# A hybrid diffusion block on one core: the seventh pair's output splits and weights one by one, the first query weights split earlier, a shorter chain in the norms

## The chip, the cores and the metric

The kernel runs on one core of a Trainium2 chip. The metric is the device time of one execution in microseconds (us). Before the change it is 1886.7 us, the median of three runs (1886.16 to 1886.85). Five engines work beside each other: TensorE (PE in the profile; its weight loads are PEld), VectorE (DVE), ScalarE (ACT), GpSimd (POOL), and the queue SP that issues the transfers.

## The reference, cut to what matters

Two layers over 512 latent tokens and a prefix of 256 context tokens, all in float32, D_MODEL 1024: attention with QK-norm, a ConvFFN, a bidirectional SSD mixer, a second ConvFFN. Ahead of each sub-layer stands an RMSNorm with shift and scale:

```python
def rms_norm(x, g):
    y = xf * lax.rsqrt(jnp.mean(xf * xf, axis=-1, keepdims=True) + EPS)
h_l = modulate(rms_norm(x, norm_mix_w[i]), mod_l[0], mod_l[1])
# attention: 16 heads of 64, 4 key-value heads; latent queries see all 768 keys, context queries 256
s = jnp.einsum('bqhgd,bkhd->bhgqk', q, k) * (HEAD_DIM ** -0.5)
p = jax.nn.softmax(s, axis=-1)
o_l = ob.reshape(bsz, seq, Q_DIM) @ w_o
x = x + mod_l[2] * o_l
x = x + mod_l[5] * conv_ffn(h_l, ffn_w_up[i], ...)
```

mod_l and mod_c come from SiLU(cond) through a linear map per layer (adaLN).

## The kernel before

**Numbers and splits.** Channels lie on partitions and tokens along the rows: a tile of X is 128 channels by 512 latent or 256 context tokens. Each float32 factor of a product is split into a high part, cast by ScalarE (`split`, L85), and a low part, the difference, taken by VectorE or GpSimd (L87). A product is three matmuls: high by high (L105), high by low activations (L106), low weights by high (L108). `load_w` fetches a weight tile of 128x1024 (wst) and splits it into wh and wl.

**Order of work.** In attention the order on TensorE, ScalarE and VectorE comes from a planner of the tile framework, which starts from the order in which the code issues the work; matmuls, casts and sums of different generators are interleaved by hand. `Fill` is a queue of generators of side work: run(us) takes from it until so many microseconds of TensorE's time are spent. `spread(us)` does the same for `stream()`, which holds ten items: four query projections for pairs 4 to 7 (`qproj`) and six blocks of adaLN products (ps_ada).

**Attention.** Sixteen heads are eight pairs. For a pair, `maxima()` makes scores in one rounding (ps_m) and takes their maxima (L610, ma, mb); from these comes a diagonal matrix diag (L631). `steps()` has seven steps, t = 0 to 6: scores ps_s (L680, with diag L682 subtracting the maxima), exp on ScalarE (pr, L683), sums of pr (acc, L688 and L690), and one step later the products with the values (ps_o, L644; in the context part ps_oc). ps_s and ps_m share a PSUM pool of two tiles, so the scores of a step wait for the exp, or the maximum, two tiles earlier. A pair ends with o = ps_o / ps_sum (L653 to L657), and pairs 0 to 5 park o in DRAM. The maxima of pair p+1 run beside the steps of pair p. `values()` is the stretch ahead of the pairs: products of v with the first maxima between them. `osplit(p)` fetches a parked o and splits it (hhol, hlol of 512 columns; hhoc, hloc of 256), and `project(fs)` multiplies it by w_o (ps_d) as side work. In the seventh pair (p = 6), at t = 0, five osplits are issued one after another, then `late()`, which loads the five w_o tiles in its projections.

**Norms.** `Norm.sq` squares a tile (L325) and adds it to one of two sums; the last tile (m = 7) adds to one (L330) and then adds the other (L332). `rstd_rows` sums over channels on TensorE (ss, L236), takes Ln and Exp on ScalarE (L241), improves the root on VectorE (L243, L244), spreads it to 128 columns per block of tokens (rb, L247) and transposes that on TensorE (rsT, L253), so that each partition has the row of roots. `Norm.gen` copies the row out of PSUM (rs, L345), and `modulated` (ht L281, hh L290, hl L291) makes the eight normed tiles of a segment of 256 tokens. Norm names: a (before attention, own code), f (before both FFNs), s (before the SSD layer). Segments: three for the first f and for s, two for the last f, eight in all.

Of the kernel before, what the change touches and what calls it, by code (L numbers as in the profile page):

```python
# [80 lines left out]
def split(g, src, hi, lo, lo_engine="dve", pin=False):  # L81

    nc = g.nc
    keep = g.tc.keep_in_program_order if pin else lambda i: i
    keep(nc.scalar.copy(hi, src))  # L85
    eng = nc.vector if lo_engine == "dve" else nc.gpsimd
    keep(eng.tensor_tensor(lo, src, _r(hi), ALU.subtract))  # L87


# [131 lines left out]


def ln_exp(g):
    follow(g, g.nc.scalar.preload_act_table_set("natural_log_exp_and_others"))


def rstd_rows(g, sq, n, cols, width, name, bank):
# [19 lines left out]
    nc.vector.scalar_tensor_tensor(rb.rearrange("p (a b) -> p a b", b=P // c), wide(u), 1.5, wide(y), ALU.add, ALU.mult)  # L247
    yield BREAK
    out = []
    for t0 in range(0, nt, 4):  # L250
        pt = bank(f"rsT{name}")
        for t in range(t0, min(nt, t0 + 4)):
            nc.tensor.transpose(pt[:, (t - t0) * P : (t - t0 + 1) * P], rb[:, t * P : (t + 1) * P], g.ident)  # L253
        yield (pt, t0 * P, min(n, (t0 + 4) * P))
# [55 lines left out]
class Norm:  # L310
# [8 lines left out]
    def sq(self, seg, x, m):  # L319

        i, a, b = seg
        nc = self.g.nc
        sq = t3(self.g, f"sq{self.name}", n=b - a)
        for ap, c0, c1 in parts(x[i][m], a, b):
            nc.scalar.activation(sq[:, c0:c1], ap, AF.Square)  # L325
# [4 lines left out]
        (nc.vector if m == 7 else nc.gpsimd).tensor_tensor(acc, acc, sq, ALU.add)  # L330
        if m == 7:
            nc.vector.tensor_tensor(acc, acc, self.acc[seg, 0], ALU.add)  # L332

    def gen(self, seg, x, lag=2):
# [7 lines left out]
        for _ in range(lag):  # L342
            yield
        rs = t3(g, f"rs{self.name}", n=n)
        nc.scalar.copy(rs, next(rows)[0][:, :n])  # L345
        for m in range(KT):
# [33 lines left out]
def attention(g, fill, X, late):  # L380
# [177 lines left out]
    qraw = {p: raw[j] for p, j in ((0, 1), (1, 2), (2, 4), (3, 5))}  # L558

    def qproj(p):  # L560

# [3 lines left out]
        w = t4(g, "wh", F32R), t4(g, "wl", F32R)  # L565
        split(g, st, *w, lo_engine="pool")
        yield
        qs = qraw[p] = t3(g, "qs")
        for h, c0, n in ((hc, L, C), (hl, 0, L)):
            ps = Bk("ps_q")  # L570
            for k in range(KT):
                ks = slice(k * P, (k + 1) * P)
                mm3(g, (w[0][:, ks], w[1][:, ks]), [(ps[:, :n], h[k])], k == 0, k == KT - 1)
                yield 3 * n / 2400
            nc.scalar.copy(qs[:, c0 : c0 + n], ps[:, :n])

    def queries(p, eng):
# [13 lines left out]
    class Pair:  # L591
# [43 lines left out]
        def steps(self):  # L635
# [37 lines left out]
            for t in range(7):  # L673
                ps, pr = Sb("ps_s"), g.t3p.tile([P, 1024], F32, tag="pr", bufs=3, name="pr")
                for q0, n, k0, off in (((0, L, t * P, 0),) if t < 6 else ((L, C, L, 0), (L, C, L + P, C))):
# [5 lines left out]
                    for e in range(2):  # L681
                        nc.tensor.matmul(outs[e], onesr[S64[e]], self.diag[S64[e], q], start=False, stop=True)  # L682
                nc.scalar.activation(pr, ps, AF.Exp)  # L683
                if t == 0:
# [34 lines left out]
    odram = [g.dp.tile([P, T], F32, name=f"odram{p}") for p in range(6)]  # L719

    def osplit(p):
        hl_, hc_ = htiles(g, L, f"ol{p}"), htiles(g, C, f"oc{p}")
        o = g.o[p]
        if p < 6:
            o = t3(g, f"od{p}")
            nc.sync.dma_start(o, odram[p])
        split(g, o[:, :L], *hl_)
        split(g, o[:, L:T], *hc_)
        g.oT.append((hl_, hc_))
# [5 lines left out]
    def stream():  # L735
# [38 lines left out]
    for i, _ in enumerate(vals):  # L774
# [4 lines left out]
        if i in (12, 26, 30, 34):  # L779
            next(qgen[2], None)  # L780
        if i == 20:
            next(side)
    for gen in (m, qgen[1], qgen[2]):
        for _ in gen:
            pass
    late_step = None
    for p in range(NH // 2):
        m = iter(())
        if p < 7:
            m = pairs[p + 1].maxima()  # L790
        if p == 6:
            for _ in side:
                pass
            for _, gen in tails:
                for _ in gen:
                    pass
        for t, todo in enumerate(pairs[p].steps()):
# [9 lines left out]
            if p == 7 and t == 3:  # L807
                osplit(5)
                osplit(6)
# [502 lines left out]
def body(nc, tc, I, out, dbg=None):  # L1312
# [37 lines left out]

    def project(fs):

        ws = [load_w(g, I["w_o"][f * P : (f + 1) * P]) for f in fs]
        yield 0
        for i in range(2):
# [3 lines left out]

    def late():  # L1360
        for fs in ((0, 1, 2), (3, 4), (5, 6, 7))[:-1]:
            fill.add(project(fs))

# [136 lines left out]
```

## Time and profile before

| | |
|---|---|
| median of three runs | 1886.7 us (1886.16 to 1886.85) |
| profiled execution | 1888.97 us |
| its span, first to last instruction | 1887.2 us |
| mean granted TensorE clock | 0.997 |
| TensorE busy | 1857.0 us, 98% |
| VectorE busy | 1315.0 us, 70% |
| ScalarE busy | 811.3 us, 43% |
| GpSimd busy | 303.5 us, 16% |
| transfers | 211.67 MB, mean 112 GB/s |

The span is what the trace covers; the execution's time also holds 1.8 us around it. The profiled execution is 2.3 us above the median. "Busy" counts the time in which an engine has an instruction in work; a busy TensorE may run at a lower granted clock (1.00 is full). A line's number is that of the kernel before; the changed kernel's lines have other numbers (L85 and L87 stay, L105 is L106, L247 is L252, L281 is L292, L610 is L625, L631 is L646, L690 is L705).

### The profile page before, as it was taken

Reading aid. Unit: us, or ns where it says so; the run is one execution under the profiler, and the core shown is the slowest. Engines: PE = TensorE matmul, PEld = TensorE weight load, DVE = VectorE, ACT = ScalarE, POOL = GpSimd, SP = SyncE. Lnnn points to the kernel's source line nnn. Section 1 sums busy time; section 2 is a strip of 40 time slices with the busy share of each in tenths; the row PEclk is TensorE's granted clock in tenths of the full one; section 3 lists DMA queues with packets and bytes.
Section 4 is the critical chain, followed back from the end, with each engine's and each line's share of the span. In section 5 each row is a group of like instructions: output and inputs, shape, how many; then the busy total and the mean of one; then the engine's idle time right before and its main releaser. Section 6 shows DMA issues by size and latency. Waiting matters only on the chain.

```text
span 1887.2 us, 28798 instructions
## 1 busy us (share of the span) xinstructions
PE 1857.0 (98%) x11474; PEld 1549.0 (82%) x11474; DVE 1315.0 (70%) x1950; ACT 811.3 (43%) x1410; POOL 303.5 (16%) x266
## 2 busy tenths in 40 slices
PE   9999999999999999999999999999999999999999
PEld 7866655688888888888888888888888888888887
DVE  6578887687877776444487877777787476565655
ACT  3534443363222222222367667776666252323331
POOL 2132120040000000000031334444333210000000
PEclk9999999999999999999999999999999999999999
DMA  9232151115434553122224324343453222323232
GB/s 342 78 117 87 63 179 50 50 41 201 140 129 140 195 176 116 55 67 68 67 90 131 117 88 117 113 124 123 123 157 105 74 95 95 101 85 106 90 101 90
DMA packets 74070, 211.67 MB, mean 112 GB/s; under 512 B 9040, under 2 KB 14544, under 8 KB 73808
## 3 DMA queue, kind: packets, MB, share of 16 engines
q1 hardware_dynamic: 73936, 209.84, 33.9%
q8 instruction: 90, 1.47, 0.3%
q14 instruction: 44, 0.36, 0.1%
HBM read 198.79 MB, written 6.82 MB: 109 GB/s over the span
## 4 chain that ended last, share of the span: by engine, by line
PE 80%; DVE 11%; issue 4%; POOL 2%; ACT 2%; DMA 1%; SPq 0%; DVEq 0%; POOLq 0%; ACTq 0%
PE ps_up L106 10%; PE ps_up L108 10%; PE ps_up L105 10%; PE ps_d L105 6%; PE ps_d L106 6%; PE ps_d L108 6%; PE ps_in L108 4%; PE ps_in L106 4%; PE ps_in L105 4%; PE ps_s L680 2%; PE ps_o L644 2%; PE ps_st L1090 1%; DVE wl L87 1%; DVE ht L281 1%; DVE xf L1020 1%
## 5 line engine op out<-in xcount | busy, mean ns | idle before, releaser
L87 DVE TENSOR_TENSOR wl<-wst,wh 128x1024 fp32r<-128x1024 f32 x207 | 261.0, 1261 | 229.9 <-PE ps_up L106 141.9
L85 ACT CAST wh<-wst 128x1024 fp32r<-128x1024 f32 x211 | 221.3, 1049 | 398.4 <-DMA wst<-in_wup 322.0
L106 PE MATMUL ps_up<-hlf,wh 128*128 128x512 f32 (+1 forms) x1008 | 357.4, 355 | 0.0
L108 PE MATMUL ps_up<-hhf,wl 128*128 128x512 f32 (+1 forms) x1008 | 357.2, 354 | 0.0
L105 PE MATMUL ps_up<-hhf,wh 128*128 128x512 f32 x1008 | 357.2, 355 | 0.0
L105 PEld LDWEIGHTS ps_up<-hhf,wh 128*128 128x128 f32 x1008 | 190.6, 189 | 26.4
L106 PEld LDWEIGHTS ps_up<-hlf,wh 128*128 128x128 f32 x1008 | 190.8, 189 | 26.2
L108 PEld LDWEIGHTS ps_up<-hhf,wl 128*128 128x128 f32 x1008 | 190.7, 189 | 26.3
L105 PE MATMUL ps_in<-hhs,wh 128*128 128x512 f32 (+1 forms) x560 | 204.6, 365 | 1.2 <-ACT dt L975 1.2
L106 PE MATMUL ps_in<-hls,wh 128*128 128x512 f32 (+1 forms) x560 | 199.6, 356 | 0.0
L108 PE MATMUL ps_in<-hhs,wl 128*128 128x512 f32 (+1 forms) x560 | 199.0, 355 | 0.0
L105 PE MATMUL ps_d<-hdh,wh 128*128 128x512 f32 (+1 forms) x568 | 193.6, 343 | 0.3 <-ACT hdh L85 0.2
L108 PE MATMUL ps_d<-hdh,wl 128*128 128x512 f32 (+1 forms) x568 | 193.5, 341 | 0.0
L106 PE MATMUL ps_d<-hdl,wh 128*128 128x512 f32 (+1 forms) x568 | 193.0, 340 | 0.3 <-DVE hdl L87 0.3
L841 DVE SCALAR_TENSOR_TENSOR X<-ps_d,mod,X 128x512 f32<-128x512 f32 (+1 forms) x224 | 124.6, 583 | 37.1 <-PE ps_d L108 36.8
L105 PEld LDWEIGHTS ps_in<-hhs,wh 128*128 128x128 f32 x560 | 106.0, 189 | 16.3 <-ACT dt L975 1.4
L106 PEld LDWEIGHTS ps_d<-hdl,wh 128*128 128x128 f32 x568 | 106.7, 188 | 14.7 <-DVE hdl L87 0.7
L108 PEld LDWEIGHTS ps_in<-hhs,wl 128*128 128x128 f32 x560 | 105.9, 189 | 14.8
L105 PEld LDWEIGHTS ps_d<-hdh,wh 128*128 128x128 f32 x568 | 106.4, 188 | 13.6 <-ACT hdh L85 0.6
L108 PEld LDWEIGHTS ps_d<-hdh,wl 128*128 128x128 f32 x568 | 106.8, 188 | 13.1
L106 PEld LDWEIGHTS ps_in<-hls,wh 128*128 128x128 f32 x560 | 106.1, 189 | 13.2
L683 ACT ACTIVATE pr<-ps_s 128x1024 f32<-128x1024 f32 x56 | 57.2, 1021 | 105.2 <-PE ps_s L682 105.1
(344 smaller groups left out, 3679.7 us busy)
## 6 DMA issues: line engine op xcount, KB each, us to landing
wst<-in_wup SPq DMA_DIRECT2D x88, 512.0 KB, 3.3
wada<-in_adaT SPq DMA_DIRECT2D x56, 512.0 KB, 3.3
wst<-in_win SPq DMA_DIRECT2D x48, 512.0 KB, 3.4
wst<-in_wdown SPq DMA_DIRECT2D x44, 512.0 KB, 3.7
E<-ad SPq DMA_DIRECT2D x64, 256.0 KB, 6.1
wada<-in_adaB SPq DMA_DIRECT2D x24, 512.0 KB, 4.4
ec<-ead SPq DMA_DIRECT2D x64, 128.0 KB, 5.5
wst<-in_wout SPq DMA_DIRECT2D x16, 512.0 KB, 3.3
```

The lines of the kernel that those rows point to most:

```text
L85: keep(nc.scalar.copy(hi, src))
L87: keep(eng.tensor_tensor(lo, src, _r(hi), ALU.subtract))
L105: mm(out, wh, ah, start=first, stop=False)
L106: mm(out, wh, al, start=False, stop=False)
L108: mm(out, wl, ah, start=False, stop=last)
L281: nc.vector.scalar_tensor_tensor(t[:, c0:c1], ap, g.moda[layer][ca][:, m, v : v + 1], rs[:, c0:c1], ALU.mult, ALU.mult)
L644: nc.tensor.matmul(po[S64[e], :n], v, pr[:, 512 * e + off : 512 * e + off + n], start=first, stop=last)
L680: nc.tensor.matmul(outs[e], kk[e][a][S64[e], k], b[S64[e], q], start=i == 0, stop=False)
L683: nc.scalar.activation(pr, ps, AF.Exp)
L841: nc.vector.scalar_tensor_tensor(ap, o[:, c0:c1], gate[:, m, v : v + 1], ap, ALU.mult, ALU.add)
L1020: i = nc.vector.scalar_tensor_tensor(cv, raw[:, tap : tap + n], par(f"sw{tap}", j), cv, ALU.mult, ALU.add)
L1090: nc.tensor.matmul(ps[:, d * 256 : (d + 1) * 256], Bt[:, t * P : (t + 1) * P], xw[d][t], start=t == ts[0], stop=t == ts[-1])
```

## The change

Three things are changed. **First**, `stream()`'s second item, the query projection of pair 4, gets its cast and its low part during the values' stretch (at i == 30; the side work is started at i == 16 instead of 20); the casts of the other three query weights are kept behind the newest exp by an ordering without a semaphore. **Second**, in pair 6 one osplit, one fetch of the next o and one w_o tile are issued per step, t = 0 to 4; the projections are added at t = 2 (three) and t = 4 (two). In pair 5 and in steps 0 to 2 of pair 6 the stream is spent with 0.62 us per step (1.04 before), what is left of it at t = 2 of pair 6; from then on Fill.run gets 3.5 us per step (2.9 before). **Third**, where a row has one column per token block (c == 1), the improved root stays 128x(blocks) and TensorE's transpose reads it as a broadcast operand; the copy out of PSUM is gone, and ht reads the row there; for m == 7 the two older sums are added before the last square.

```diff
@@ split
-    keep(nc.scalar.copy(hi, src))
+    cast = keep(nc.scalar.copy(hi, src))
...
+    return cast
...
+def behind(g, bi, other):
+    g.tc.add_manual_dep(bi.ins, other.ins.name, mybir.DependencyInfo(
+        mybir.DependencyClass.NoSync, mybir.DependencyReason.DATA), reason="kept behind")
...
@@ rstd_rows
-    rb = t3(g, f"rb{name}", n=n)
-    wide = lambda v: v.unsqueeze(2).broadcast_to([P, nt * c, P // c])
-    nc.vector.scalar_tensor_tensor(rb.rearrange("p (a b) -> p a b", b=P // c), wide(u), 1.5, wide(y), ALU.add, ALU.mult)
+    if c == 1:
+        nc.vector.scalar_tensor_tensor(a, u, 1.5, y, ALU.add, ALU.mult)
+        root = lambda t: a[:, t : t + 1].broadcast_to([P, P])
+    else:
...
-            nc.tensor.transpose(pt[:, (t - t0) * P : (t - t0 + 1) * P], rb[:, t * P : (t + 1) * P], g.ident)
+            nc.tensor.transpose(pt[:, (t - t0) * P : (t - t0 + 1) * P], root(t), g.ident)
@@ Norm.sq, Norm.gen
-        (nc.vector if m == 7 else nc.gpsimd).tensor_tensor(acc, acc, sq, ALU.add)
         if m == 7:
             nc.vector.tensor_tensor(acc, acc, self.acc[seg, 0], ALU.add)
+        (nc.vector if m == 7 else nc.gpsimd).tensor_tensor(acc, acc, sq, ALU.add)
...
-        rs = t3(g, f"rs{self.name}", n=n)
-        nc.scalar.copy(rs, next(rows)[0][:, :n])
+        rs = next(rows)[0][:, :n]
@@ attention, qproj
-        split(g, st, *w, lo_engine="pool")
+        cast = split(g, st, *w, lo_engine="pool")
+        if exps:
+            behind(g, cast, exps[-1])
@@ attention, osplit and the values' stretch
+    def ofetch(p):
+        od[p] = t3(g, f"od{p}")
+        nc.sync.dma_start(od[p], odram[p])
...
-            if i + 1 < len(items) and i + 1 in (1, 3, 4, 5):
+            if i + 1 in (3, 4, 5):
                 next(items[i + 1])
...
-        if i == 20:
+        if i == 16:
             next(side)
+        if i == 30:
+            next(items[1])
@@ attention, the pairs
-        if p == 6:
-            for _ in side:
-                pass
...
-            if t == 0:
-                if p == 6:
-                    for i in range(5):
-                        osplit(i)
-                    late()
...
-                spread(1.04)
+                    if p == 5:
+                        ofetch(0)
+                spread(1.04 if p < 5 else 0.62)
+                continue
+            if p == 6 and t < 5:
+                if t < 4:
+                    ofetch(t + 1)
+                osplit(t)
+                wos.append(load_w(g, I["w_o"][t * P : (t + 1) * P]))
+            if p == 6 and t == 2:
+                late(wos[:3], (0, 1, 2))
+            if p == 6 and t == 4:
+                late(wos[3:], (3, 4))
+            if p == 7 and t == 2:
+                ofetch(5)
...
+            if p == 6 and t < 3:
+                spread(0.62)
+                if t == 2:
+                    for _ in side:
+                        pass
...
             else:
-                fill.run(2.9)
+                fill.run(3.5)
```

**GpSimd at the start of the pairs.** Three ropes (L534 to L536 before, L544 to L546 now; raw_901 before and raw_899 now are the sixth tile of raw queries and keys) and the low parts wl of the query weights. Before, three wl in a row stand behind the third rope:

```order
L534 TENSOR_TENSOR raw_903<-raw_903,cs 128x512
L535 TENSOR_TENSOR qsw<-qsw,cs 128x512
L536 TENSOR_TENSOR raw_903<-raw_903,qsw 128x512
L87 TENSOR_TENSOR wl<-wst,wh 128x1024 x3
L534 TENSOR_TENSOR raw_901<-raw_901,cs 128x512
```

Now:

```order
L87 TENSOR_TENSOR wl<-wst,wh 128x1024
L544 TENSOR_TENSOR raw_901<-raw_901,cs 128x512
L545 TENSOR_TENSOR qsw<-qsw,cs 128x512
L546 TENSOR_TENSOR raw_901<-raw_901,qsw 128x512
L544 TENSOR_TENSOR raw_899<-raw_899,cs 128x512
```

The first wl moved ahead of a rope, and two wl stand behind the last rope of raw.

**VectorE around the seventh pair's diag.** accc is the sum of pair 5's last exp, mz the smaller of the maxima, od a fetched o. Before:

```order
L694 TENSOR_TENSOR accc<-pr 128x512
L626 TENSOR_TENSOR mz<-ma,mb 64x6 x4
L87 TENSOR_TENSOR wl<-wst,wh 128x1024
L631 TENSOR_TENSOR diag_3262<-id_918,mz 128x6x64 x2
L655 TENSOR_TENSOR o_2939<-ps_o,y 128x512
L656 SCALAR_TENSOR_TENSOR u<-ps_sum,y 128x512
L610 TENSOR_REDUCE ma<-ps_m 128x2x2
```

Now:

```order
L709 TENSOR_TENSOR accc<-pr 128x512
L641 TENSOR_TENSOR mz<-ma,mb 64x6 x4
L646 TENSOR_TENSOR diag_3223<-id_916,mz 128x6x64 x2
L87 TENSOR_TENSOR hlol_3316<-od_3238,hhol_3315 128x512
L670 TENSOR_TENSOR o_2937<-ps_o,y 128x512
L671 SCALAR_TENSOR_TENSOR u<-ps_sum,y 128x512
L133 STREAM_TRANSPOSE ada_tr<-ps_ada 128x128
L672 SCALAR_TENSOR_TENSOR o_2937<-u,o_2937 128x512
L87 TENSOR_TENSOR hloc_3318<-od_3238,hhoc_3317 128x256
L87 TENSOR_TENSOR hlol_3351<-od_3313,hhol_3350 128x512
L625 TENSOR_REDUCE ma<-ps_m 128x2x2
```

The wl ahead of diag is gone from there, and two low parts of o and an adaLN transpose now stand between diag and the next maximum.

**ScalarE in the last segment's norm before the second FFN.** Before:

```order
L325 ACTIVATE sqf_14796<-x_13858 128x256
L85 CAST wh<-wst 128x1024
L241 ACTIVATE rsy<-rsa 128x2
L241 ACTIVATE rsy<-rsy 128x2
L345 COPY rsf_14842<-rsTf_14843 128x256
L290 ACTIVATE hhf_0_14371<-ht,mod_95 128x256
```

Now:

```order
L336 ACTIVATE sqf_14772<-x_13838 128x256
L247 ACTIVATE rsy<-rsa 128x2
L85 CAST wh<-wst 128x1024
L247 ACTIVATE rsy<-rsy 128x2
L301 ACTIVATE hhf_0_14350<-ht,mod_95 128x256
```

The weight cast moved from ahead of Ln to between Ln and Exp, and the copy is gone.

More of the change, by code (lines that the diff above doesn't have):

```diff
@@ L244, in rstd_rows @@
     nc.vector.scalar_tensor_tensor(u, y, -0.5, u, ALU.mult, ALU.mult)
-    rb = t3(g, f"rb{name}", n=n)
-    wide = lambda v: v.unsqueeze(2).broadcast_to([P, nt * c, P // c])
-    nc.vector.scalar_tensor_tensor(rb.rearrange("p (a b) -> p a b", b=P // c), wide(u), 1.5, wide(y), ALU.add, ALU.mult)
+    if c == 1:
+        nc.vector.scalar_tensor_tensor(a, u, 1.5, y, ALU.add, ALU.mult)
+        root = lambda t: a[:, t : t + 1].broadcast_to([P, P])
+    else:
+        rb = t3(g, f"rb{name}", n=n)
+        wide = lambda v: v.unsqueeze(2).broadcast_to([P, nt * c, P // c])
+        nc.vector.scalar_tensor_tensor(rb.rearrange("p (a b) -> p a b", b=P // c), wide(u), 1.5, wide(y),
+                                       ALU.add, ALU.mult)
+        root = lambda t: rb[:, t * P : (t + 1) * P]
     yield BREAK
-    out = []
     for t0 in range(0, nt, 4):
@@ L558, in attention @@
     qraw = {p: raw[j] for p, j in ((0, 1), (1, 2), (2, 4), (3, 5))}
+    exps = []
     def qproj(p):
@@ L575, in qproj @@
             nc.scalar.copy(qs[:, c0 : c0 + n], ps[:, :n])
+        qraw[p] = qs
     def queries(p, eng):
@@ L682, in steps @@
                         nc.tensor.matmul(outs[e], onesr[S64[e]], self.diag[S64[e], q], start=False, stop=True)
-                nc.scalar.activation(pr, ps, AF.Exp)
+                exps.append(nc.scalar.activation(pr, ps, AF.Exp))
                 if t == 0:
@@ L815, in attention @@
                         pass
-                spread(1.04)
+                    if p == 5:
[13 more added lines that the diff above has]
+                ofetch(5)
+            if p == 7 and t == 3:
+                osplit(5)
+                osplit(6)
+            if p == 6 and t < 3:
[3 more added lines that the diff above has]
+                        pass
+                    for _, gen in tails:
+                        for _ in gen:
+                            pass
             else:
-                fill.run(2.9)
+                fill.run(3.5)
     late_step()
@@ L1349, in body, with project @@
     x = [[X[:, m, a:b] for m in range(KT)] for a, b in ((0, L), (L, T))]
-    def project(fs):
-        ws = [load_w(g, I["w_o"][f * P : (f + 1) * P]) for f in fs]
-        yield 0
+    def project(fs, ws):
         for i in range(2):
@@ L1358, in project, with late @@
                 yield 3 * len(fs) * streams[i][0] / 2400
-    def late():
-        for fs in ((0, 1, 2), (3, 4), (5, 6, 7))[:-1]:
-            fill.add(project(fs))
+    def late(ws, fs):
+        fill.add(project(fs, ws))
     attention(g, fill, X, late)
```

14 lines of the change are left out of this document (3 added, 11 removed).

## The prediction

> **What bounds the kernel now.** First the page's totals of busy time, then the windows table (span cut into stretches; columns: length, busy time of TensorE's matmuls, its weight loads, VectorE, ScalarE and GpSimd with their counts, granted TensorE clock, DMA share, GB/s):
>
> ```profile
> span 1887.2 us, 28798 instructions
> PE 1857.0 (98%) x11474; PEld 1549.0 (82%) x11474; DVE 1315.0 (70%) x1950; ACT 811.3 (43%) x1410; POOL 303.5 (16%) x266
> 110.00:130.00 20.00, 18.12 (x168) 12.35 (x167) 14.96 (x16) 6.86 (x10) 9.25 (x5) 0.91 0.51 172
> 130.00:258.00 128.00, 128.00 (x930) 77.67 (x929) 102.46 (x146) 57.58 (x80) 24.98 (x14) 1.00 0.23 74
> 258.00:310.00 52.00, 46.81 (x424) 27.81 (x422) 47.00 (x79) 24.92 (x38) 4.80 (x3) 0.97 0.46 164
> 385.00:435.00 50.00, 47.99 (x361) 45.04 (x360) 39.88 (x83) 30.56 (x69) 19.18 (x23) 1.00 0.26 95
> 930.00:990.00 60.00, 55.74 (x435) 52.53 (x435) 43.98 (x97) 36.95 (x85) 20.99 (x25) 1.00 0.23 80
> 1500.00:1530.00 30.00, 26.24 (x207) 24.43 (x205) 21.66 (x45) 14.35 (x34) 4.60 (x5) 1.00 0.21 70
> ```
>
> TensorE is the bound: 98% over the span, no gap at all in 130 to 258. So what TensorE gains early reaches the end, and the change can win only where TensorE idles: 1.9 us in 110 to 130, 5.2 in 258 to 310, 2.0 in 385 to 435, 4.3 in 930 to 990, 3.8 in 1500 to 1530. The clock column holds more: it is below 1 in just two of these rows. Cut finer:
>
> ```profile
> 122.00:124.00 2.00, 2.00 (x12) 0.57 (x8) 1.02 (x2) 1.66 (x2) 1.13 (x1) 0.59 0.01 4
> 124.00:126.00 2.00, 2.00 (x8) 1.22 (x7) 2.00 (x2) 0.00 (x0) 1.22 (x1) 0.56 0.01 4
> 292.00:294.00 2.00, 1.71 (x8) 0.80 (x8) 2.00 (x4) 1.02 (x1) 0.00 (x0) 0.76 0.00 0
> 294.00:296.00 2.00, 2.00 (x5) 1.00 (x6) 1.86 (x5) 0.80 (x2) 0.00 (x0) 0.50 0.01 4
> 296.00:298.00 2.00, 2.00 (x12) 0.91 (x10) 1.40 (x4) 0.84 (x1) 0.00 (x0) 0.89 0.05 20
> ```
>
> The first two rows lose 2x(0.41+0.44) = 1.7 us to the slow clock, the other three 2x(0.24+0.50+0.11) = 1.7 us. TensorE counts as fully busy there, so no wait shows this cost. Each stretch follows a stall, so a stall's price can be its idle time plus 1.7 us.
>
> **Part A, the first query weights.** Timeline rows (start, length, engine; idle before and releaser in brackets):
>
> ```profile
> 113.94 1.28 POOL L534 TENSOR_TENSOR raw<-raw,cs 128x512 f32<-128x512 f32 x1 [13.03 <-ACT pr L683]
> 118.58 2.34 POOL L87 TENSOR_TENSOR wl<-wst,wh 128x1024 fp32r<-128x1024 f32 x1
> 118.81 0.28 PE L106 MATMUL ps_q<-hla,wh 128*128 128x256 f32 x1
> 120.97 0.39 PE L108 MATMUL ps_q<-hha,wl 128*128 128x256 f32 x1 [1.88 <-POOL wl L87]
> ```
>
> GpSimd does a rope (three operations from 113.94 on) first and the low part wl behind it. The changed order puts wl ahead of that rope, and its cast into the values' stretch, where GpSimd had been idle for 13.03 us. Then the wait goes: 120.97-118.81 = 2.16 us from start to start, less the product's own 0.28: 1.9. The slow clock behind it goes too, since no other wait is listed in 110 to 130: 1.7. **A = 3.6.** Lower bound 1.1: the clock loss stays, and wl at its new place costs VectorE something; nearest is the operation that it ends up beside (VectorE's diag of 1.02 us, below, doubled at worst, of which I count 0.8). Nothing else waits for the casts pushed behind the last exp: TensorE has no idle time in 130 to 258.
>
> [...]
>
> **Part B, pairs six and seven of the eight (258 to 310).** The rows in order of time; the first is pair six's diag part of the scores, the second the end of pair five's ctx sums:
>
> ```profile
> 260.05 0.50 PE L682 MATMUL ps_s<-diag,onesr 64*128 64x512 f32 x2 [0.71 <-DVE diag L631]
> 261.63 0.60 PE L650 MATMUL ps_oc<-accc,ones 128*64 128x256 f32 x4
> 266.83 1.08 PE L644 MATMUL ps_o<-pr,v 128*64 128x512 f32 x4
> 269.19 1.08 PE L644 MATMUL ps_o<-pr,v 128*64 128x512 f32 x4
> 270.20 1.95 PE L129 MATMUL ps_ada<-wada,sc 128*32 128x128 f32 x64
> 282.02 0.50 PE L608 MATMUL ps_m<-khs,qh 64*128 64x512 f32 x1 [1.17 <-DVE ma L610]
> 285.27 0.38 PE L680 MATMUL ps_s<-qh,kh 64*128 64x256 f32 x1 [1.74 <-ACT pr L683]
> 290.07 1.23 DVE L87 TENSOR_TENSOR wl<-wst,wh 128x1024 fp32r<-128x1024 f32 x1
> 291.21 1.02 DVE L631 TENSOR_TENSOR diag<-id,mz 128x384 fp32r<-128x384 f32 x2
> 292.29 0.50 PE L682 MATMUL ps_s<-diag,onesr 64*128 64x512 f32 x2 [1.57 <-DVE diag L631]
> 294.35 1.22 PE L105 MATMUL ps_d<-hhol,wh 128*128 128x512 f32 x2
> 296.05 0.68 DVE L87 TENSOR_TENSOR hlol<-od,hhol 128x512 fp32r<-128x512 f32 x1
> ```
>
> VectorE sets the pace here: 47.00 of 52 us busy. A wide operation takes 1.14 from start to start (290.07 to 291.21), 0.09 less than its length; a step takes TensorE 2.36 when nothing waits (266.83 to 269.19). The change takes wl from in front of the seventh pair's diag and puts one adaLN block (1.95) ahead of that pair's first scores. So the diag wait, 1.57, goes. The block at 270.20 is the one that moves, so both engines can run up to 1.95 earlier from there and the wait for ma falls from 1.2 to about 0.6; the wait for pr stays at 1.7 to 1.9, because its exp stands behind a cast that waits for VectorE. With the part of the slow clock before 294.35 (0.7) and the spacings around the stalls, my schedule by hand has the ctx sums end at 290.7 instead of 294.35: 3.6 earlier.
>
> Behind that the cost comes. The products with w_o (ps_d), which filled TensorE between the seventh pair's steps, now stand behind the scores of step 3. In its new order VectorE must do, from diag to the maximum that step 3 waits for: 3 maxima, 2 sums and one wl (6 at 1.14 = 6.8); three hlol, a last one excepted, and three rows of o, u, o of 512 columns (6 at 0.6, from hlol's 0.68 = 3.6); three hloc and three rows of 256 (6 at 0.34, hloc's 0.42 below = 2.0); small ones 0.6: 13.0 us. TensorE has for it 2.2, from the diag part to the end of the ctx sums (260.05 to 262.23, one pair earlier), and three steps of 2.36, 9.3 in all, of which 0.5 follows the last wait. New idle time: 13.0-8.8 = 4.2. Before, between 294.35 and 304.65, TensorE did 24 ps_d (5.5 at full clock) and one step (2.4), 7.9 us of work in 10.3: it lost 2.4 there. So 3.6-4.2+2.4 = 1.8. I take off half of one slow stretch (0.85 to 0.9), as three gaps of 1.1 to 1.7 follow each other within 10 us. **B = 0.9.** Bounds: -1.6 (two slow stretches, 3.4) and +6.2 (waits of 1.2+1.7+1.6 and the clock's 1.7 all gone, none new). The fetches of o and the w_o loads come one per step instead of all at once; at over 2.36 us a step they stay hidden behind the step before.
>
> **Part E, end of attention.**
>
> ```profile
> 379.74 0.42 DVE L87 TENSOR_TENSOR hloc<-o,hhoc 128x256 fp32r<-128x256 f32 x1
> 380.21 0.38 PE L106 MATMUL ps_d<-hloc,wh 128*128 128x256 f32 x1 [0.63 <-DVE hloc L87]
> ```
>
> The larger filling per step (3.5 for 2.9) and the earlier projection put one group of 24 ps_d more behind the last sums, each of 0.1 us at least, which is over three times the wait. **E = 0.6**, bounds 0 and 0.8 (a second small wait stands before it).
>
> **Part N, the norms.** First the row of the kernel's first norm, then the last segment before the second FFN, which shows the whole chain:
>
> ```profile
> 15.04 0.69 DVE L247 SCALAR_TENSOR_TENSOR rba<-rsu,rsy 128x512 f32<-128x512 f32 x1
> 1520.68 0.42 DVE L330 TENSOR_TENSOR sqf<-sqf,sqf 128x256 f32<-128x256 f32 x1 [0.48 <-ACT sqf L325]
> 1521.14 0.42 DVE L332 TENSOR_TENSOR sqf<-sqf,sqf 128x256 f32<-128x256 f32 x1
> 1522.33 0.16 DVE L239 TENSOR_SCALAR rsa<-ssf 128x2 f32<-128x2 f32 x1 [0.76 <-PE ssf L236]
> 1523.55 0.15 DVE L243 TENSOR_TENSOR rsu<-rsy,rsa 128x2 f32<-128x2 f32 x1
> 1524.01 0.43 DVE L247 SCALAR_TENSOR_TENSOR rbf<-rsu,rsy 128x256 f32<-128x256 f32 x1
> 1525.03 0.37 ACT L345 COPY rsf<-rsTf 128x256 f32<-128x256 f32 x1 [2.07 <-PE rsTf L253]
> 1525.43 1.28 DVE L281 SCALAR_TENSOR_TENSOR ht<-x,moda,rsf 128x256 f32<-128x256 f32 x3 [1.00 <-ACT rsf L345]
> 1526.51 0.50 PE L105 MATMUL ps_first<-hhf,wh 128*128 128x256 f32 x2 [1.52 <-ACT hhf L290]
> ```
>
> One addition leaves the chain (0.46, start to start), rb shrinks to a 128x2 operation (0.43 to 0.16, as rsa: 0.27), and the copy goes (1525.03 to 1525.43: 0.40): 1.1 us per exposed chain. TensorE shows no product from a broadcast operand; nearest is the same transpose of rb, bounds 0 and +0.3 each, and I take 0. Exposed are the last segments of three norms, eight segments in all; the others run under the segment ahead. Before the first FFN **+0.9** (of 2.0 us idle), before the SSD layer **+0.9** (of 4.3, of which another wait, ps_in for dt, isn't touched). Before the second FFN ScalarE now does a weight cast between Ln and Exp, and the wl that needs this cast stays ahead of rsu on VectorE: from rsa's end at 1522.49 on, Ln, a cast about as long as wl, and wl (1.14) put rsu near 1525.0 instead of 1523.55, so 1.1-1.4: **-0.3**. The first norm's 512-wide rb (0.69) shrinks too: **+0.4**, bounds 0 and 0.5. **N = 1.9**, bounds -2 and 4.
>
> **Sum.** 3.6+0.9+0.6+1.9 = 7.0 us. The profiled execution took 1888.97 us (span 1887.2), 2.27 above the median of 1886.7; it would take 1882.0, the median **1879.7**.
>
> **Rivals.** *Rival 1, the stalls only move:* in pair seven VectorE stays the bound and two slow stretches fall there: B = -1.6; with N at 0, the gain is 3.6-1.6+0.6 = 2.6, 1884.1. For it: 47 of 52 us of VectorE. Against: A alone doesn't depend on it. *Rival 2, everything clears:* B = 6.2, gain 12.3: 1874.4. For it: the fill moved is as long as the stalls. Against: the VectorE count above. [...] *Rival 4, slower:* rs is no longer copied out, so its PSUM bank is held until the eighth ht has read it, 8x0.40 = 3.2 us instead of 0.4; the next segment's sum ssf stands behind that on TensorE's queue, and the ps_first and ps_d products behind ssf. At 1.4 us lost in each of the eight segments N is -11.2, and with A+B+E = 5.1 the time is 1892.8; it comes out slower by 3.8 from (5.1+3.8)/8 = 1.1 us a segment on. For it: ssf did move down TensorE's order. Against: VectorE takes ssf up late anyway, there are four such banks, and the eight ht of the row at 1525.43 follow each other as fast as VectorE lets them, whichever memory rs lies in.
>
> **How the numbers follow.** Forecast 0.62 (own range 1876.5 to 1882.9), rival 1 0.18, rival 2 0.08, rival 3 0.07, rival 4 0.05. About 0.2%, 3.8 us, is what a measurement of this kernel can tell from no change, so faster is below 1882.9: most of the forecast (0.57), rival 2, rival 3's better part (0.05): 0.70. Same: rival 1, the rest of the forecast and of rival 3, 0.25. Slower 0.05. Range 1874.5 to 1885.5, from near rival 2 past rival 1.
>
> **What would show it.** A: no wait of ps_q for GpSimd's wl, and clock 1.00 in 118 to 126. B: the diag wait under 0.3 in the seventh pair; three waits of ps_m for ma of 1.1 to 1.7 before the first ps_d; sums 3 us earlier relative to the scores of pair five. E: no wait for hloc near the end of attention. N: ps_first's last-segment waits shorter by about 1 us before the first FFN and the SSD layer, not before the second FFN. Wrong would be: a clock below 1 in 110 to 130, TensorE waits with ssf, or pair seven's gaps over 6 us.

## The result, and the profile after

The changed kernel takes **1876.4 us** (median of four runs, 1874.7 to 1879.2) where the kernel before takes 1886.6 in runs beside it: a ratio of 0.9946, 95% interval 0.993 to 0.9962, 10.1 us less. Forecast were 7.0 less and 1879.7, range 1874.5 to 1885.5. The sign and the range held; the gain came out 1.45 times as large, and by the parts it is not the forecast gain: one part gave a third of what was expected, another more than twice. The profiled execution of the changed kernel took 1875.1 us; of it, the page's totals of busy time, and then the windows table:

```profile
span 1873.4 us, 28794 instructions
...
PE 1847.5 (99%) x11474; PEld 1544.9 (82%) x11474; DVE 1301.8 (69%) x1950; ACT 807.8 (43%) x1402; POOL 301.7 (16%) x266
```

```profile
110.00:130.00 20.00, 20.00 (x186) 13.50 (x188) 14.80 (x18) 7.00 (x11) 4.69 (x4) 1.00 0.46 159
130.00:258.00 128.00, 127.28 (x934) 77.05 (x930) 105.07 (x152) 59.50 (x84) 28.41 (x15) 1.00 0.28 89
258.00:310.00 52.00, 47.39 (x428) 27.81 (x429) 47.42 (x72) 24.06 (x35) 5.71 (x3) 0.97 0.41 137
385.00:435.00 50.00, 48.44 (x347) 45.17 (x346) 42.42 (x85) 29.32 (x60) 13.59 (x16) 1.00 0.34 122
930.00:990.00 60.00, 56.61 (x427) 53.35 (x426) 49.09 (x106) 34.36 (x80) 19.85 (x25) 1.00 0.23 77
1490.00:1520.00 30.00, 27.06 (x211) 25.19 (x211) 23.24 (x49) 14.97 (x34) 5.15 (x6) 1.00 0.23 74
```

TensorE works without a gap at full clock in 110 to 130, where it idled 1.88 us and had clock 0.91. GpSimd's first low part is now ahead of the last rope, as the order had it, and the wait of ps_q for it is gone (timeline rows of GpSimd):

```profile
108.51 2.40 POOL L87 TENSOR_TENSOR wl<-wst,wh 128x1024 fp32r<-128x1024 f32 x1 [7.60 <-PE ps_v L531]
110.87 1.28 POOL L544 TENSOR_TENSOR raw<-raw,cs 128x512 f32<-128x512 f32 x1
```

In the pairs (255 to 315) the big diag wait of 1.57 is gone too, and small waits for the maxima stand in its place (what TensorE's matmuls waited for: total, times, longest):

```profile
PE ps_m L623 <- DVE ma L625: 2.9, 4, 1.0
PE ps_s L695 <- ACT pr L698: 1.7, 1, 1.7
PE ps_s L697 <- DVE diag L646: 0.7, 1, 0.7
```

**Idle time shows a third of it.** Between the two profiles TensorE's idle time falls by 4.6 us in the five stretches of the forecast (1.9 in 110 to 130, 0.6 in 258 to 310, 0.5 in 385 to 435, 0.9 in 930 to 990, 0.8 in 1490 to 1530), while the span falls by 13.8. Two stretches of slow clock less account for up to 3.4. The rest is in how a stall is shown. TensorE's timeline of the kernel before, at one stall in the first feed-forward:

```profile
422.39 0.28 PE L105 MATMUL ps_first<-hhf,wh 128*128 128x256 f32 x1
422.51 0.28 PE L106 MATMUL ps_first<-hlf,wh 128*128 128x256 f32 x1
423.26 0.39 PE L106 MATMUL ps_first<-hlf,wh 128*128 128x256 f32 x1 [0.47 <-DVE hlf L291]
423.48 0.40 PE L108 MATMUL ps_first<-hhf,wl 128*128 128x256 f32 x2
```

Undisturbed, such a product starts 0.12 after the one ahead of it, and is shown 0.28 long. From 422.51 to 423.26 are 0.75 us, so 0.63 are lost, and 0.10 more on the way to 423.48, the next start: 0.73, for an idle time of 0.47. So this stall costs 0.26 us more than its row (the wait of 1.88 us in A, by the account below, 2.1 us), and by these numbers one under 0.16 us (0.28 less 0.12) has no row.

So a better account is wanted: each product is given the spacing that its shape has undisturbed (the median in the changed kernel's trace: 0.120 us at 256 columns, 0.227 at 512, 0.111 at a transpose), and what a start comes later than that is **lost**. Cut where an equal amount of TensorE's work is done, stretches of two kernels can be compared even where their products run in another order. All kernels lose the same in the long feed-forward part, to 0.01 us, so the account is fine enough for tenths, where the executions themselves don't differ. Lost time, us, of one profiled execution each, against the kernel before (the pairs' column reaches to the end of attention, so E is in it; the start is all work ahead of A):

| kernel | start | A | pairs, end of attention | norm, first FFN | norm, SSD | norm, second FFN | elsewhere | slow clock from (us) |
|---|---|---|---|---|---|---|---|---|
| before | 0 | 0 | 0 | 0 | 0 | 0 | 0 | 20, 122, 293 |
| after | -1.25 | -4.21 | -3.54 | -1.77 | -1.73 | -1.24 | -0.10 | 278 |
| A only | -0.87 | -1.24 | -1.69 | 0.03 | 0.03 | 0.17 | -0.07 | 19, 115 |
| B and E only | -0.47 | -1.69 | -3.73 | 0.09 | 0.05 | 0.00 | -0.67 | 20 |
| norms only | -0.73 | -2.81 | -1.92 | -1.65 | -1.47 | -0.32 | -0.53 | 1516 |
| gap filled | -1.03 | -3.24 | -1.16 | 0.04 | -0.25 | 0.21 | -0.56 | 15, 281 (twice as long) |
| copy put back | -0.99 | -1.27 | -4.13 | 0.47 | 0.49 | 0.52 | 0.64 | 19, 114 |
| casts behind root | -0.88 | -4.14 | -3.63 | -1.77 | -1.57 | -3.61 | 0.01 | 19, 278 |
| exp before cast | -1.10 | -4.14 | -5.99 | -1.76 | -1.30 | -1.23 | 0.49 | 15 |
| filling of 2.9 | -0.85 | -4.21 | -4.03 | -1.77 | -1.44 | -1.25 | -0.05 | 20 |
| old adds | -1.23 | -1.10 | -3.97 | -2.48 | 0.03 | -1.75 | -0.01 | 115 |
| wide root | -0.03 | -4.14 | -3.77 | -1.45 | -1.28 | -2.85 | -0.25 | 20, 279 |
| both orders | -0.29 | -4.21 | -6.17 | -1.77 | -1.43 | -3.59 | -0.20 | 20 |
| adds by norm | -0.59 | -3.02 | -5.92 | -2.50 | -1.46 | -3.75 | -0.21 | none |

The kernel before had an unlucky profiled execution (three slow stretches): A only, which touches nothing in the pairs, stands 1.7 below it there. So columns are read against the kernels without the edit, not against zero.

### The profile page after: what moved, and what is told of

It is laid out like the page before. It is cut to its first block, busy times and chain, and to the rows that moved or that the text cites. A ratio compares the mean times of both kernels' runs of the same rounds, so it can differ in the third digit from the quotient of the medians.

```text
span 1873.4 us, 28794 instructions
## 1 busy us (share of the span) xinstructions
PE 1847.5 (99%) x11474; PEld 1544.9 (82%) x11474; DVE 1301.8 (69%) x1950; ACT 807.8 (43%) x1402; POOL 301.7 (16%) x266
## 3 DMA queue, kind: packets, MB, share of 16 engines
q8 instruction: 90, 1.47, 0.3%
## 4 chain that ended last, share of the span: by engine, by line
PE 83%; DVE 8%; issue 3%; ACT 2%; DMA 2%; POOL 1%; SPq 0%; DVEq 0%; POOLq 0%; ACTq 0%
PE ps_up L107 10%; PE ps_up L109 10%; PE ps_up L106 10%; PE ps_d L106 6%; PE ps_d L109 6%; PE ps_d L107 6%; PE ps_in L109 4%; PE ps_in L107 4%; PE ps_in L106 4%; PE ps_s L695 2%; PE ps_o L659 2%; PE ps_st L1121 2%; PE ps_wo L109 1%; PE ps_wo L106 1%; PE ps_wo L107 1%
## 5 line engine op out<-in xcount | busy, mean ns | idle before, releaser
L107 PE MATMUL ps_up<-hlf,wh 128*128 128x512 f32 x1008 | 357.0, 354 | 0.0
L109 PE MATMUL ps_up<-hhf,wl 128*128 128x512 f32 x1008 | 356.8, 354 | 0.0
```

Source lines behind the costliest of these rows:

```text
L107: mm(out, wh, al, start=False, stop=False)
L109: mm(out, wl, ah, start=False, stop=last)
```

## The parts one by one

Each kernel here is the one before with one part of the change.

**A only:** the first query weights split in the values' stretch, the others' casts behind an exp.

> Only the first change (query weights of pair 4 split in the values' stretch, the other casts kept behind the exps). My theory: the wait of 1.9 us and the slow clock of 1.7 us behind it both go, 3.6 us faster, 1882.9. Rival (the slow clock has another cause and comes again): 1.9 us faster, 1884.6. If the parts are not independent (the trace of the changed kernel shows 3.75 us at this place), a clearly different number.

1885.0 us (10 runs) against 1886.2: ratio 0.9993, interval 0.9984 to 1.0003. At 0.6 us more to 3 us less, this isn't the 3.6 of the forecast. Its windows show why:

```profile
110.00:130.00 20.00, 19.35 (x176) 13.51 (x176) 14.97 (x17) 5.19 (x8) 5.57 (x4) 0.91 0.49 172
114.00:116.00 2.00, 2.00 (x41) 1.97 (x44) 1.76 (x5) 0.43 (x2) 1.92 (x3) 0.67 1.07 389
116.00:118.00 2.00, 2.00 (x38) 1.60 (x32) 1.92 (x3) 0.00 (x0) 0.79 (x1) 0.50 0.92 367
```

The wait for wl has gone, and the clock still drops, ahead of the place where the stall was. And a new wait has come ahead of it, of the first scores for their diag (rows of VectorE, GpSimd and TensorE):

```profile
109.00 3.22 DVE L642 TENSOR_TENSOR diag<-id,mz 128x384 fp32r<-128x384 f32 x2
109.31 2.49 POOL L87 TENSOR_TENSOR wl<-wst,wh 128x1024 fp32r<-128x1024 f32 x1 [9.29 <-PE ps_v L527]
112.28 0.50 PE L693 MATMUL ps_s<-diag,onesr 64*128 64x512 f32 x2 [0.65 <-DVE diag L642]
```

The two halves of diag took 3.22 us here beside the wl that the change moved to this place, and 1.02 in the profile of the changed kernel; TensorE loses 0.9 us by it. Copy put back, old adds and adds by norm have the same wait, the other six kernels with A have not.

**B and E only:** the seventh pair's steps, the spread of the stream, the larger filling.

> Only the second change (output splits and w_o one by one, spread 0.62, fill 3.5). The prediction's terms: B 0.9 and E 0.6, 1.5 us faster, 1885.0. By the trace of the changed kernel (2.1 up to the end of the seventh and eighth pairs, 1.45 in the tail of attention): 3.5 us faster, 1883.0, and up to 5.2 where no slow-clock stretch falls into pair six.

1883.5 us (10 runs): 0.9985, interval 0.9975 to 0.9994, 2.8 us less. TensorE's wait for wl in A is there unchanged (1.9 us), yet no slow stretch follows it in the profiled execution.

**Norms only:** narrow root, order of the adds, no copy.

> Only the third change (norms). The prediction's term: 1.9 us faster, 1884.6. By the trace of the changed kernel (1.25 at the first norm, 1.8 before the first FFN, 1.6 before the SSD layer, 1.2 before the second FFN): 5.9 us faster, 1880.6. The rival that held the PSUM bank against it: slower than 1886.5.

1881.1 us (7 runs): 0.9974, interval 0.9963 to 0.9985, 4.9 us less, half of the whole gain. The three parts alone sum to 1.3+2.8+4.9 = 9.0, beside the 10.1 of all of them together.

## Is the slow clock the stall's doing?

**Gap filled:** the kernel before, with 14 more products of the same form in A's gap (into unused columns of the bank: work without use, which changes no output).

```diff
+ for _ in range(14):
+     nc.tensor.matmul(ps[:, n : 2 * n], w[0][:, ks], h[k][0], start=False, stop=False)
```

> The kernel before with 14 useless products of 256 columns (into unused columns of ps_q's bank) between the second and the third product of ps_q, in the gap in which TensorE waits for GpSimd's wl. The wait for wl itself stays. If idle time in that gap causes the slow clock behind it: the clock stays at 1.00 in 122 to 126 and the kernel is 1.7 us faster, 1884.8. If the slow clock has another cause: no change, 1886.5.

1886.2 us (10 runs): 0.9999, interval 0.9989 to 1.0008, so 2.1 us less to 1.5 more: the 1.7 us of a slow stretch are neither shown nor excluded. Its profiled execution has no slow stretch here, but it was no full test either (rows of GpSimd and TensorE):

```profile
115.70 2.39 POOL L87 TENSOR_TENSOR wl<-wst,wh 128x1024 fp32r<-128x1024 f32 x1
119.19 0.28 PE L578 MATMUL ps_q<-hha,wl 128*128 128x256 f32 x1
```

wl was done at 118.09, where the kernel before has it at 120.92. The third product would have waited some 0.6 us; the 14 products (1.7 us, 14x0.12) kept it until 119.19, 1.1 longer than needed.

So the stall itself is not in every execution, though GpSimd's order is the same. Its rope ahead of wl waits for a fetch (qsw<-raw). In six profiled executions (before, A only, B and E only, copy put back, old adds, adds by norm) this fetch was issued late, where TensorE had done 91.0 us of its work by the account, and in the other eight where it had done 89.4 to 90.7. Without A, the late ones wait 1.9 us for wl (before, B and E only); norms only, an early one, has no wait for wl, but one of 1.1 for a maximum. With A, the late ones have the diag wait above and the early ones none. Compared like with like, A is worth 1.3 us both ways: -3.02 (adds by norm) against -1.69 (B and E only), and -4.14 to -4.21 against -2.81 (norms only).

What the traces have of it: a slow stretch lasts 3.41 us (or twice that), and within one execution all of them start on one grid of 3.413 us. Before, 19.96, 122.36 and 293.02 lie 30 and 50 such steps apart, to 0.01. Between executions the grid shifts (19.96 and 122.36 in the one, 19.09 and 114.67 in another). That it depends also on a stall's place on this grid whether a slow stretch follows is an estimate; no run shows it. In the profile of the changed kernel it happened here:

```profile
276.00:278.00 2.00, 0.27 (x4) 0.27 (x6) 2.00 (x2) 2.00 (x3) 0.00 (x0) 1.00 1.01 300
278.00:280.00 2.00, 2.00 (x22) 1.78 (x22) 2.00 (x3) 1.03 (x2) 0.00 (x0) 0.52 0.99 390
280.00:282.00 2.00, 2.00 (x6) 0.59 (x8) 1.99 (x5) 0.62 (x1) 0.00 (x0) 0.63 0.41 164
```

In the 3.41 us ahead of it TensorE was busy for a share of 0.49. Ahead of the others in these profiles it was 0.41 to 0.64, and 0.81 to 0.84 ahead of the three that start at 114.4 to 114.9 us; in the kernel before, a step of the grid with 0.49 (up to 286.20) was not followed by one, and in the changed kernel one with 0.52 (up to 1513.69). So the share that the profile shows as busy doesn't decide it alone, and what does stays open. Those three stand in executions with the diag wait (A only, copy put back, old adds). Adds by norm has that wait without a slow stretch, and none of the six kernels with A but without the wait has one there: a stall seems to take part, and no stall brings it for certain. The longest single idle time of TensorE in the 3.41 us ahead of a slow stretch of the table was 1.88 us in the kernel before (ahead of 122.36) and 1.74 in the changed one (ahead of 278.06).

What a slow stretch costs depends on the place too. In the pairs, with B in, it costs 0.3: kernels without it stand at -3.73 to -4.13, those with it at -3.54 to -3.77; TensorE waits there for VectorE anyway (3.6 us in the rows of the changed kernel above).

## Why the norms gave more than twice the forecast

**Copy put back:** the changed kernel, with this one edit undone.

```diff
-        rs = next(rows)[0][:, :n]
+        rs = t3(g, f"rs{self.name}", n=n)
+        nc.scalar.copy(rs, next(rows)[0][:, :n])
```

> The changed kernel with ScalarE's copy of the row of roots put back (ht reads the copy, the PSUM bank is free after it). My theory: the copy and its hop are 0.4 us of each exposed chain, so the stretches before the first FFN, the SSD layer and the second FFN each get 0.3 to 0.5 us longer, about 1.2 us in all. Rival (a held bank costs time): these stretches get shorter, by more than 0.2 us each.

1883.0 us (10 runs): 0.9987 of the time before, interval 0.9978 to 0.9997. All of the norms' gain is gone: against the changed kernel the three norms lose 2.2, 2.2 and 1.8 us, and stand 0.5 each above before. So the copy alone is worth 6.2 us in this kernel (6.6 by the medians). The forecast had 0.40 for it per chain, its length on the path. VectorE's rows for the multiplication that reads the rows of roots, around the first feed-forward norm, from the groups (busy, mean ns, idle before) and from the tile's page (min/median/max ns, first and last start). Before:

```profile
L281 DVE SCALAR_TENSOR_TENSOR ht<-X,moda,rsf 128x256 f32<-128x256 f32 x24 | 12.0, 530 | 2.2 <-ACT rsf L345 2.2
```

```profile
L281 DVE SCALAR_TENSOR_TENSOR ht<-X,moda,rsf x24: 468/474/959, 393.0 to 423.1; 128x256 f32<-128x256 f32 x24
```

After:

```profile
L292 DVE SCALAR_TENSOR_TENSOR ht<-X,moda,rsTf 128x256 f32<-128x256 f32 x24 | 10.5, 472 | 0.9 <-PE rsTf L264 0.9
```

```profile
L292 DVE SCALAR_TENSOR_TENSOR ht<-X,moda,rsTf x24: 462/472/483, 383.3 to 412.6; 128x256 f32<-128x256 f32 x24
```

With the copy put back:

```profile
L292 DVE SCALAR_TENSOR_TENSOR ht<-X,moda,rsf 128x256 f32<-128x256 f32 x24 | 13.3, 589 | 2.3 <-ACT rsf L356 2.3
```

```profile
L292 DVE SCALAR_TENSOR_TENSOR ht<-X,moda,rsf x24: 468/477/959, 386.8 to 417.4; 128x256 f32<-128x256 f32 x24
```

Two things go with the copy. VectorE waits 0.9 us for the transposes around this norm, where it waited 2.2 for the copy. And with the roots in PSUM no ht takes longer than 0.483 us; with the roots copied to SBUF some take up to twice as long: 0.79 to 0.98 us in 8 of the 64 in the three norms before (four more took 0.57) and in 15 of 64 with the copy put back. Every one of these 23 starts while GpSimd is at an operation (sums of squares, or a low part) and ends 0.28 us after it; an ht that starts ahead of the GpSimd operation keeps its length (0.47 to 0.48 us before, where no other was under way), and then the GpSimd operation ends 0.60 to 1.00 us after the ht. In the changed kernel 22 ht overlap such an operation too and none takes longer than 0.483. In all the 64 take 34.1 us before, 30.2 after and 37.4 with the copy back. What in this overlap makes an ht longer, the runs don't show. How much of the 6.2 us is the wait and how much the longer ht, no run here separates.

**Old adds** and **wide root:** the changed kernel, each with one of the other two edits undone.

```diff
         acc = self.acc[seg, 6 if m == 7 else 0]
+        (nc.vector if m == 7 else nc.gpsimd).tensor_tensor(acc, acc, sq, ALU.add)
         if m == 7:
             nc.vector.tensor_tensor(acc, acc, self.acc[seg, 0], ALU.add)
-        (nc.vector if m == 7 else nc.gpsimd).tensor_tensor(acc, acc, sq, ALU.add)
```

> The changed kernel with the two adds of the squares in the order of before (the last square first, the half sums behind it); the copy stays away and the root stays narrow. With the copy put back (the run ahead of this one) the three norms of the body lost 6.1 us against the changed kernel and stood 1.5 us above before. Theory 1: what counts is the copy on ScalarE, with its wait in that queue; the order of the adds is worth 0 to 0.5 us a norm, so the time is 1876 to 1878 and the three norm stretches stay within 1.5 us of the changed kernel's. Rival: the three edits work only together, since the add that is due last sets the root as much as the copy sets what follows it; then 2 us or more a norm come back and the time is 1880 to 1883.

1876.4 us (5 runs), 0.9949, interval 0.9935 to 0.9963: nothing lost in all, but not because the order is idle. The old order is 0.7 us better before the first feed-forward, 0.5 better before the second, and takes the whole 1.7 us gain before the SSD layer away.

```diff
-    if c == 1:
+    if c == 0:
         nc.vector.scalar_tensor_tensor(a, u, 1.5, y, ALU.add, ALU.mult)
```

> The changed kernel with the wide root (256 columns, 0.43 us on VectorE against 0.16) put back in the norms; the copy stays away and the new order of the adds stays. Theory 1 (the copy carries the gain): the root's chain grows by 0.27 us in each of two segments, part of it hidden; the time is 1876 to 1878. Rival (the edits work only together): 1880 to 1883. A third way: the narrow root costs something by itself, as the run with the copy put back hints, which stood 1.5 us above before; then this kernel is faster than the changed one, 1873.5 to 1875.5.

1877.7 us (5 runs), 0.9954, interval 0.9941 to 0.9966. The narrow root is worth 0.3 us before the first feed-forward and some 0.4 before the SSD layer, and costs 1.6 before the second feed-forward. The copy carries the norms' gain, as the theory had it; the two small edits move it between places.

**Casts behind the root,** in the last norm alone. What the forecast said of the slip there, the changed kernel's trace has; ScalarE and then VectorE:

```profile
1507.88 0.20 ACT L247 ACTIVATE rsy<-rsa 128x2 f32<-128x2 f32 x1 [1.41 <-DVE rsa L245]
1507.98 1.03 ACT L85 CAST wh<-wst 128x1024 fp32r<-128x1024 f32 x1
1508.92 0.20 ACT L247 ACTIVATE rsy<-rsy 128x2 f32<-128x2 f32 x1
```

```profile
1507.68 0.16 DVE L245 TENSOR_SCALAR rsa<-ssf 128x2 f32<-128x2 f32 x1 [0.76 <-PE ssf L242]
1509.05 1.22 DVE L87 TENSOR_TENSOR wl<-wst,wh 128x1024 fp32r<-128x1024 f32 x1 [1.21 <-ACT wh L85]
1510.19 0.15 DVE L249 TENSOR_TENSOR rsu<-rsy,rsa 128x2 f32<-128x2 f32 x1
```

From rsa to rsu are 2.51 us, 1.22 before. The edit keeps each weight cast behind the norm's Exp, and each low part on VectorE behind the finished root, by ordering without a semaphore.

```diff
@@ split
+    if getattr(g, "root", None):
+        behind(g, cast, g.root)
...
+    if getattr(g, "rootv", None) and lo_engine == "dve":
+        behind(g, low, g.rootv)
```

> The changed kernel with the weight casts of the last norm kept behind its Exp, and their low parts behind its root on VectorE. My theory: the slip of rsu (2.5 us after rsa, 1.2 before the change) is the cast and wl between them; without it the stretch before the second FFN gets 1.2 us shorter. Rival: wl, late now, holds the first products of the FFN and gives it back, 0.

1873.35 us (4 runs): 0.9935, interval 0.992 to 0.995, and in its stretch alone 2.4 us less than the changed kernel, twice the slip that was expected back, since the root now comes 0.67 us after rsa:

```profile
1507.23 0.16 DVE L249 TENSOR_SCALAR rsa<-ssf 128x2 f32<-128x2 f32 x1 [0.76 <-PE ssf L246]
1507.90 0.16 DVE L256 TENSOR_TENSOR rsu<-rsy,rsa 128x2 f32<-128x2 f32 x1 [0.51 <-ACT rsy L251]
```

## The pairs, and a kernel that beats both

**Filling of 2.9** per step in place of 3.5, the rest as changed.

> The changed kernel with 2.9 us of side work per step instead of 3.5 from the seventh pair's fourth step on. If the gain of 1.6 us at attention's end (hhoc's and hloc's waits gone, and the last segments' projection reached earlier) comes from the larger filling: those 1.6 us come back. If it comes from the projections being added earlier: no change.

1876.7 us (4 runs), 0.9954, interval 0.9937 to 0.997; the pairs' column is no worse than the changed kernel's (-4.03 against -3.54, which has a slow stretch). E doesn't come from the larger filling. By elimination it comes from the projection that is added earlier, which no run takes away alone: in the column's last part, the end of attention, the changed kernel loses 0.4 where the one before loses 2.0, and kernels without B and E are as before.

**Exp before cast:** pair eight's query cast kept behind the newest exp, since an exp stood behind it in ScalarE's queue while TensorE waited 1.7 us for pr.

```diff
-        split(g, qs, *qprep[p])
+        cast = split(g, qs, *qprep[p])
+        if p == 7:
+            behind(g, cast, exps[-1])
```

> The changed kernel with the cast of the eighth pair's qh kept behind the exp that it stood ahead of. The planner also puts a wl back in front of the seventh pair's diag. My theory: the wait of 1.7 us of the scores for pr goes, but the stretch is bound by VectorE, so other waits take it up and the pairs end at most 0.8 us earlier; a run that would have had a slow-clock window there gains 1.7 more. Rival: 1.7 us shorter up to the end of attention.

1874.7 us (4 runs), 0.9942, interval 0.9927 to 0.9957. Its waits of TensorE in 255 to 315:

```profile
PE ps_m L625 <- DVE ma L627: 2.2, 3, 1.1
PE ps_s L699 <- DVE diag L648: 2.1, 2, 1.4
PE ps_s L697 <- ACT pr L700: 0.6, 1, 0.6
```

The wait for pr fell by 1.1, part of it came back as a diag wait, and the stretch is 2 us better than in kernels with B that have no slow stretch there, where at most 0.8 was expected. Beside the changed kernel's 1876.4 the time of this one edit isn't told apart.

**Both orders** together:

> The changed kernel with both fixed orders at once: casts behind the root in the last norm (1873.35 alone), pair eight's query cast behind the exponential (1874.66 alone); the changed kernel took 1876.41. If the two gains stand in different stretches and add up: 1876.4 - 3.05 - 1.75 = 1871.6. If the second was only a profile and runs with fewer slow stretches of the clock: the first one's 1873.3.

**1870.7 us** (4 runs, 1869.95 to 1871.31): 0.9919, interval 0.9905 to 0.9932. The two gains stand in different stretches (-6.17 and -3.59 in the table) and add up; every run of it lies below every run of the changed kernel. **Adds by norm,** the old order of the adds in the two feed-forward norms on top:

> Both fixed orders (1870.7), and the adds of the squares in the new order before the SSD layer only; the two feed-forward norms take the old order. By stretches the old order was 0.7 us better before the first feed-forward, 1.4 worse before the SSD layer and 0.5 better before the second. If stretches can be set one by one: 1870.7 - 0.7 = 1870.0, or 1869.5 if the second norm's half us is had on top of its fixed casts. If the planner's later order is changed by the first norm's: 1870.5 to 1872, with a stretch elsewhere that loses.

1870.4 us (5 runs, 1869.6 to 1871.5): 0.9913, interval 0.9899 to 0.9926. The first norm's stretch takes the old order's value (-2.50), the SSD norm keeps its own (-1.46), the second feed-forward's gets 0.2 more. The 0.3 us to the kernel ahead is less than a measurement tells.

## Why the prediction was right, and where its terms were not

- **A, 3.6 = wait 1.9 + clock 1.7, measured 1.3** (interval -0.6 to 3.0). Both steps were too large. The wait for wl does go, as forecast, but in late executions the wait for diag comes in its place, and in early ones the full wait was not there to be won. The forecast had this second price, wl beside VectorE's diag, in its lower bound of 1.1 alone, and 1.1 is near what came. The step "the slow clock behind it goes too" failed: there is a wait of 1.9 us without a slow stretch (B and E only), and the clock is below 1 in 110 to 130, the sign that the forecast itself had named, in three of ten profiled executions with A. Rival 3, which put A at its wait alone (1.9, so 1881.4), was nearer there. The row of "each stretch follows a stall" was read off two stretches of one execution (which has a third, at 19.96, that the forecast didn't look at), and one execution cannot tell a cause from a phase.
- **B, 0.9.** The mechanism was right: the diag wait went, maxima wait in its place (four waits for ma). Its size came from two misses that cancel. The three gaps in pair seven were 0.2, 1.0 and 0.9, 2.1 us in all, where the count of VectorE's work had 4.2; and the ctx sums end at 287.24, 7.1 earlier than before, of which the start and A gave 5.3, so 1.8 and not 3.6. In kernels without a slow stretch there, B and E together give 4.0-1.8 = 2.2, and E 1.6 of it: B is 0.6.
- **E, 0.6, measured 1.6.** Right in sign; the term took the idle of 0.63 for the stall's price, and set it partly on the larger filling, which has no share in it.
- **N, 1.9, measured 4.9** (interval 2.8 to 7.0). By place 0.9 became 1.8, 0.9 became 1.3 to 1.7, -0.3 became +1.2, and the first norm's +0.4 can't be seen (the start varies by 1.2 between profiles, with and without N). The step that failed is the copy's 0.40, and in it the sentence that ht goes as fast as VectorE lets it "whichever memory rs lies in": in SBUF one ht in eight took 0.79 to 0.96 us in place of 0.47. The slip in the last norm did happen, 1.3 us as counted, but what else the copy had cost was larger there than the slip.
- **Sum.** A 2.3 and B 0.3 too much, the norms 3.0 and E 1.0 too little: 7.0-2.3-0.3+3.0+1.0 = 8.4, and 10.1 measured; the 1.7 between is within what the runs tell. That the number held is partly luck: errors of both signs met.
- **Rivals.** Rival 1 (stalls only move) fell: no loss in pair seven. Rival 2 (everything clears, 1874.4) came near the time but not by its reason: 5.3 us of waits remain in the pairs, and the surplus came from the norms. Rival 4 (the bank held) fell: TensorE has no wait with ssf in the changed kernel, and the reads out of PSUM were shorter, not longer (the 64 ht took 30.2 us, 34.1 before).

## What to carry to other kernels

A stall on TensorE cost more than its idle row here (0.73 us for a row of 0.47, 2.1 for one of 1.88), so count stalls as well as their length; and compare two kernels by lost spacing at equal work, which shows tenths of a microsecond where medians of ten runs tell some two apart. Before putting a price on a copy that leaves PSUM, look at the maximum of the operations that read it, not at their median: a duration that doubles beside another engine's work (ht, 0.47 to 0.96 us) is a price the chain doesn't show. Give a part of the gain to a wait or a clock drop only after several executions have shown it at the same place: A's wait of 1.9 us stands in two of the four profiled executions without A. And when work moves to GpSimd, look at what VectorE does beside it at its new place: in A only two diag took 3.22 us there, 1.02 in the profile of the changed kernel.

## What the runs showed of the hardware that was not expected

- VectorE's 128x256 product of two SBUF tiles took up to 0.98 us where a GpSimd operation was under way (all 23 of 0.79 us and more), and never over 0.483 with one of the tiles in PSUM. Two diag took 3.22 us beside GpSimd's wl of 2.49 (A only), and 1.02 in the changed kernel, where wl started 0.37 after their end.
- Within an execution TensorE's slow stretches start on a grid of 3.413 us, which shifts between executions (19.96 before, 19.09 in A only), and the 3.41 us ahead of one were 0.41 to 0.64 busy, three times 0.81 to 0.84. Over 28 runs of the kernel before its time lay between 1883.6 and 1889.4 us; the profiled executions of all kernels here hold none to three such stretches while TensorE still has work (one of them twice as long), and one of 3.41 us at half clock is 1.7 us of work.
- A transpose that reads one column as a broadcast operand costs TensorE no more than one of 128 columns (0.272 against 0.300 us, medians in the SSD norm of after and before).
